# Decode attention over a paged cache: SyncE transfers with page numbers in registers instead of GpSimd's indirect gathers

## The chip, the cores and the metric

The kernel runs on one core of a Trainium2 chip. The metric is the device time of one execution in microseconds. The core has TensorE (PE; its weight loads are PEld), VectorE (DVE), ScalarE (ACT), GpSimd (POOL) and SyncE (SP). SP computes nothing; it issues transfers to the core's 16 DMA engines. Each engine runs its own instructions strictly in the order in which the program holds them.

## The reference

One inference step of a one-layer decoder: a half-step SwiGLU, a token mixer of four GLA heads and four MLA heads, a second SwiGLU. It runs over 1024 prompt tokens and over 8 sample tokens, each with 4096 past tokens in a paged cache. The change concerns the attention of the sample tokens:

```python
past_lat = cache_kv[l, page_table].reshape(B_s, -1, MLA_KV_RANK)   # page: 128 tokens x 128 f32
past_pe = cache_pe[l, page_table].reshape(B_s, -1, MLA_ROPE)       # page: 128 tokens x 64 f32
...
s = (jnp.einsum('bqhc,bkc->bhqk', q_lat, lat_all)
     + jnp.einsum('bqhr,bkr->bhqk', q_pe, pe_all)).astype(jnp.float32) * MLA_SCALE
p = jax.nn.softmax(s, axis=-1)
o_lat = jnp.einsum('bqhk,bkc->bqhc' ...)                           # then w_uv
```

`page_table` has 8 rows of 32 page numbers, drawn from a pool of 320 pages. The sum over past tokens doesn't depend on their order.

## The kernel before, in words

All large products run on TensorE in split precision (`mm3`, L88 to L95, three matmuls for one). The stages follow each other: first SwiGLU, input projection and GLA, attention, output projection (`project`, L1453, which loads w_out by L171), second SwiGLU.

The sample attention is cut into 16 decode units `(g, u)`: group g holds four of the eight sample tokens, u one of eight slices of 512 past tokens. `dec_unit` (L1165) takes four tiles `kvt` (128 partitions x 4 x 128) and four `pet` (128 x 4 x 64), one pair per sample token, from `fetch`; transposes pet (L1176) and kvt (L1184) on TensorE; computes scores (L1189, L1192), softmax (L1162, L1163), the transposes of the probabilities (L1198) and the product with kvt (L1203), which is the last use of kvt. After the units 7 and 15 (counted 0 to 15) `dec_combine` joins the slices, and L1417 applies w_uv.

Tiles come from pools. `bufs=6` at kvt and pet means six buffers for each, so that one unit and half of the next fit; a transfer into a buffer waits for the last reader of what it held.

`decode(2)` issues units 0 and 1 before the prompt attention. Then each of four heads loads its weights (`uqr`, `ukr`, L1289 and L1333, one buffer each), and computes four query blocks: `scores(m)`, then `outputs` of the block before, then `decode(1)`. So each head has four slots, and 14 units fill them. A scheduler of the framework sets the final order of each engine's instructions when the program is built; it moves them past each other where data allows, by priority, free buffers and its own estimates of durations. On the chip the order is fixed. SP's transfers take eight semaphores in turn, and each waits for the one that held its semaphore before, eight transfers back.

Before the change the tiles are filled by `indirect_dma_start` on GpSimd: a tile `idx`, made by DVE (L900 to L902), holds for each of the 128 partitions the row of the cache to fetch. A row is four tokens, and a unit takes such rows from all 32 pages.

Of the kernel before, what the change touches and what calls it, by code (L numbers as in the profile page):

```python
# [10 lines left out]
F32 = mybir.dt.float32  # L11
F32R = mybir.dt.float32r
BF = mybir.dt.bfloat16
I32 = mybir.dt.int32
U8 = mybir.dt.uint8
AF = mybir.ActivationFunctionType
OP = mybir.AluOpType
# [4 lines left out]
P = 128  # L22
# [3 lines left out]
NS = 8  # L26
# [9 lines left out]
PAST = 4096  # L36
NPOOL = 320
# [31 lines left out]
def hybrid_step(ctx: ExitStack, tc: tile.TileContext, I, O, C):  # L69
    nc = tc.nc  # L70
    V, S, PE, GP = nc.vector, nc.scalar, nc.tensor, nc.gpsimd
    ld = nc.sync

    def pool(name, bufs=1, **kw):
        cm = tc.tile_pool(name=name, bufs=bufs, **kw)
        return cm, cm.__enter__()
# [20 lines left out]
    const = ctx.enter_context(tc.tile_pool(name="const", bufs=1))  # L97
# [360 lines left out]
    tiles = [(t * P, P, I["x_prompt"][0, t * P:(t + 1) * P, :]) for t in range(8)] + [(SEQ, NS, I["x_sample"][:, 0, :])]  # L458
# [240 lines left out]
    def bank(name="ps"):  # L699
        return ps.tile([P, 512], F32, name=name, tag="ps")  # L700
# [7 lines left out]
    def mbank():  # L708
        nw[0] += 1
        return (psw, psw, psx)[nw[0] % 3].tile([P, 512], F32, name="pw", tag="pw")  # L710
# [101 lines left out]
    for s in BLKS:  # L812
        n = s.stop - s.start
# [39 lines left out]
    p = bank().rearrange("p (h x) -> p h x", h=8)  # L853
# [4 lines left out]
    for t in range(2):  # L858
        rope(pr, "ropew", qrs[:, t], qs_n[:, 4 + t], P, ss)
        for hh in range(2):  # L860
            a = slice(64 * hh, 64 * hh + 64)
            V.tensor_copy(qpp[0][:64, :, 2 * t + hh], qrs[a, t])
            V.tensor_copy(qpp[1][64:, :, 2 * t + hh], qrs[a, t])
    for h in range(4):
        p = bank()
# [25 lines left out]
    J = 4  # L891
    NU = PAST // (P * J)

    pt = const.tile([P, NS], I32, name="pt")
    for r in range(4):
        ld.dma_start(pt[r:P:4, :], I["page_table"].rearrange("b g -> g b"))
    kb = const.tile([P, NU], I32, name="kb")
    ld.dma_start(kb, C["keybase"])
    idx = const.tile([P, NU, NS], I32, name="idx")
    for u in range(NU):  # L900
        V.tensor_scalar(idx[:, u], pt, P // J, None, op0=OP.mult)
        V.tensor_tensor(idx[:, u], idx[:, u], kb[:, u:u + 1].to_broadcast([P, NS]), op=OP.add)  # L902
    newmask = const.tile([P, 2 * NS], F32, name="newmask")
    ld.dma_start(newmask, C["newmask"])
    kv_rows = I["cache_kv"].rearrange("o n (r k) c -> (o n r) (k c)", k=J)
    pe_rows = I["cache_pe"].rearrange("o n (r k) c -> (o n r) (k c)", k=J)
    fetched = {}

    def fetch(g, u, tiles=None):

        kvt, pet = tiles or ([ep.tile([P, J, P], F32, name="kvt", tag="kvt", bufs=6) for _ in range(4)],
                             [ep.tile([P, J, 64], F32, name="pet", tag="pet", bufs=6) for _ in range(4)])
        for bi in range(4):
            off = bass.IndirectOffsetOnAxis(ap=idx[:, u, 4 * g + bi:4 * g + bi + 1], axis=0)
            for t_, rows in ((kvt[bi], kv_rows), (pet[bi], pe_rows)):
                GP.indirect_dma_start(out=t_.rearrange("p j c -> p (j c)"), out_offset=None, in_=rows, in_offset=off)
        return kvt, pet

    nq = [0]
# [57 lines left out]
    def gla_norm(src, n, gk, tag="on"):  # L977

        ss = gk.tile([P, 8], F32, name="gss", tag="gss")
        on = gk.tile([P, 4, P], F32, name="on", tag=tag, bufs=1)  # L980
        for h in range(4):
            S.activation(on[:n, h], src[:n, h], AF.Square, accum_out=ss[:n, h:h + 1])
        V.tensor_scalar(ss[:n, :4], ss[:n, :4], 1.0 / P, EPS, op0=OP.mult, op1=OP.add)
        GP.tensor_tensor(ss[:n, 4:], ss[:n, :4], mhalf[:n, :4], op=OP.pow)
        for h in range(4):
            if h % 2:
                V.tensor_scalar_mul(on[:n, h], src[:n, h], ss[:n, 4 + h:5 + h])
            else:
                S.activation(on[:n, h], src[:n, h], AF.Copy, scale=ss[:n, 4 + h:5 + h])
        p = bank().rearrange("p (h i) -> p h i", h=4)  # L990
        for h in range(4):
            PE.transpose(p[:, h, :n], on[:n, h], ident[:n, :n])
        return p
# [45 lines left out]
    for c in range(2):  # L1039
# [10 lines left out]
        for t in range(9):  # L1050
            n = P if t < 8 else NS
            ts = slice(t * P, t * P + n)
            p = mbank()
# [66 lines left out]
    p = bank().rearrange("p (h v) -> p h v", h=4)  # L1120
    for h in range(4):
        PE.transpose(p[:NS, h], osn[:, h], ident)
    p = gla_norm(p, NS, gk)
# [23 lines left out]
    def dbank(name="pd"):  # L1147
        return psd.tile([P, 512], F32, name=name, tag="pd")
# [4 lines left out]
    e_cm, ep = pool("dec", 2, side="right")  # L1153
# [6 lines left out]
    def softmax(g, u, sc, n, pout):  # L1160
        stat = grp[g][0]
        V.tensor_reduce(stat[:, 0, u:u + 1], sc[:, :n], AX.X, OP.max, negate=True)  # L1162
        S.activation(pout[:, :n], sc[:, :n], AF.Exp, bias=stat[:, 0, u:u + 1], accum_out=stat[:, 1, u:u + 1])  # L1163

    def dec_unit(g, u):  # L1165

        if u == 0:
            grp[g] = (ep.tile([P, 3, NU + 1], F32, name="stat", tag="stat"), ep.tile([P, NU + 1, P], F32, name="oc", tag="oc", bufs=1))
        oc = grp[g][1]
        kvt, pet = fetched.pop((g, u)) if (g, u) in fetched else fetch(g, u)  # L1170
        sc = dbank("dsc")
        lt, pe = [], []
        for b2 in range(2):
            p = dbank()
            for q in range(4):
                PE.transpose(p[:, q * P:(q + 1) * P],  # L1176
                             pet[2 * b2 + q // 2][:, 2 * (q % 2):2 * (q % 2) + 2, :].rearrange("p j c -> p (j c)"), ident)
            peT = ep.tile([P, 512], F32, name="peT", tag="peT")
            V.tensor_copy(peT, p)
            pe += [peT[:, :256], peT[:, 256:]]  # L1180
        for bi in range(4):
            p = dbank()
            for q in range(4):
                PE.transpose(p[:, q * P:(q + 1) * P], kvt[bi][:, 2 * (q % 2) + q // 2, :], ident)  # L1184
            lt.append(ep.tile([P, 512], F32, name="latT", tag="latT", bufs=4))
            S.activation(lt[bi], p, AF.Copy)
        rows = [slice(32 * bi, 32 * bi + 32) for bi in range(4)]
        for bi in range(4):
            PE.matmul(sc[rows[bi], :], qlp[:, 4 * g + bi], lt[bi], start=True, stop=False)  # L1189
        for par in range(2):  # L1190
            for bi in range(4):
                PE.matmul(sc[rows[bi], par * 256:par * 256 + 256], qpp[par][:, 4 * g + bi], pe[bi], start=False, stop=par == 1)  # L1192
        pp = ep.tile([P, 512], F32, name="dpp", tag="dpp")
        softmax(g, u, sc, 512, pp)
        pT = ep.tile([P, J, P], F32, name="dpT", tag="dpT")
        p = dbank()
        for q in range(4):
            PE.transpose(p[:, q * P:(q + 1) * P], pp[:, q * P:(q + 1) * P], ident)  # L1198
        V.tensor_copy(pT.rearrange("p j q -> p (j q)"), p)
        po = dbank()  # L1200
        for j in range(J):
            for bi in range(4):
                PE.matmul(po[rows[bi], :P], pT[:, (j % 2) * 2 + j // 2, rows[bi]], kvt[bi][:, j], start=j == 0, stop=j == J - 1)  # L1203
        V.tensor_copy(oc[:, u], po[:, :P])
# [42 lines left out]
    def decode(n):  # L1247

        for g, u in units[:n]:
            dec_unit(g, u)  # L1250
            if u == NU - 1:
                dec_combine(g)
        del units[:n]
# [43 lines left out]
    for t in range(2):  # L1297
# [4 lines left out]
        for s in (slice(0, 512), slice(512, SEQ)):  # L1302
            p = bank()
# [3 lines left out]
            for hh in range(2):  # L1307
                a, c = slice(64 * hh, 64 * hh + 64), slice(64 - 64 * hh, 128 - 64 * hh)
# [11 lines left out]
        for j in range(8):  # L1320
            js = slice(j * P, (j + 1) * P)
            p = bank()[:, :256]
# [4 lines left out]
        for hh in range(2):  # L1327
# [9 lines left out]
            for b in range(2):  # L1337
                s = slice(b * 512, b * 512 + 512)
                p = bank()
# [75 lines left out]
    for h in range(4):  # L1415
        p = dbank()
# [23 lines left out]
    for h in range(4):  # L1440
        raw = rawp.tile([P, SEQ], F32, name="yraw", tag="raw")
        i, o = ((2, 0), (2, 256), (2, 512), (2, 768))[h]
# [225 lines left out]
```

## Time and profile before

| | |
|---|---|
| median of three runs | 2166.68 us (2166.26 to 2172.05) |
| the profiled execution | 2166.21 us |
| its span, first to last instruction | 2164.4 us |
| PE busy | 2060.4 us, 95% |
| DVE, ACT, POOL busy | 69%, 39%, 9% |
| transfers issued by SP | 223.35 MB, 33.5% of the engines' time |
| GpSimd's gathers | 25.17 MB, 3.7% |
| mean granted TensorE clock | 0.977 |

Times are microseconds from the first instruction. The busy share of an engine is a mean over stages that differ; a stage is read by its own stretch. "A <- B" in a row of waits means that A stood idle and B's end released it. A granted clock of 1 is 2.4 GHz, the lower of the two levels is 1.2 GHz.

### The profile page before, as it was taken

How to read it: one execution, taken by the hardware profiler on the slowest of the kernel's cores; microseconds unless marked ns; L12 is line 12 of the kernel's file. 1: busy time of each engine (PE TensorE's matmuls, PEld its weight loads, DVE VectorE, ACT ScalarE, POOL GpSimd, SP SyncE). 2: the span in 40 equal slices, each digit the busy share in tenths (PEclk: the TensorE clock that was granted, in tenths of full speed). 3: DMA queues.
4: the chain of work that ended last, by engine and by line, in shares of the span. 5: the costliest groups of instructions: out<-in, count | busy, mean ns of one | idle time of the engine just before them, and what ended most of it. 6: DMA issues, size and time to landing. Idle time of an engine off the chain costs nothing.

```text
span 2164.4 us, 40540 instructions
## 1 busy us (share of the span) xinstructions
PE 2060.4 (95%) x16379; PEld 1934.6 (89%) x16379; DVE 1488.0 (69%) x2918; ACT 841.7 (39%) x1563; POOL 190.7 (9%) x223
## 2 busy tenths in 40 slices
PE   9999999999999999898788888899999999999997
PEld 9999999999999988886456556799999999999997
DVE  7977777785878566664545545577777777776776
ACT  7323223243445223354533534344332232333434
POOL 0000000000000012113343331000000000000000
PEclk9999999999999999998899989999999999999999
DMA  6233233376445221032332232643332332575352
GB/s 215 72 117 94 88 114 93 95 251 208 137 130 150 74 72 30 21 98 79 112 92 81 91 100 62 190 148 113 108 90 88 118 94 86 148 259 168 109 153 94
DMA packets 202220, 251.13 MB, mean 116 GB/s; under 512 B 20240, under 2 KB 162768, under 8 KB 202032
## 3 DMA queue, kind: packets, MB, share of 16 engines
q1 hardware_dynamic: 193840, 223.35, 33.5%
q0 software_dynamic: 8192, 25.17, 3.7%
q8 instruction: 129, 2.11, 0.4%
q14 instruction: 59, 0.48, 0.1%
HBM read 189.18 MB, written 59.30 MB: 115 GB/s over the span
## 4 chain that ended last, share of the span: by engine, by line
PE 86%; DVE 4%; issue 3%; ACT 2%; DMA 2%; POOL 1%; another core or an unknown queue 1%; POOLq 0%; ACTq 0%; DVEq 0%; SPq 0%
PE pp L94 42%; PE pp L410 18%; PE pw L94 6%; PE pr L94 4%; PE pd L1184 2%; PE po L94 1%; PE dsc L1189 1%; PE pw L1059 1%; PE dsc L1192 1%; PE pg L957 1%; PE ps L94 1%; PE pd L1203 1%; DVE qt L953 1%; DMA kvt<-in_cache_kv_dram,idx 1%; PE ps L1399 1%
## 5 line engine op out<-in xcount | busy, mean ns | idle before, releaser
L94 PE MATMUL pp<-bl,ah 128*128 128x260 f32 (+1 forms) x2432 | 688.7, 283 | 1.4 <-DVE bl L86 1.4
L94 PE MATMUL pp<-bh,al 128*128 128x260 f32 (+1 forms) x2432 | 689.4, 284 | 0.2 <-DVE al L86 0.2
L94 PE MATMUL pp<-bh,ah 128*128 128x260 f32 (+1 forms) x2432 | 687.9, 283 | 0.9 <-ACT ah L85 0.5
L94 PEld LDWEIGHTS pp<-bh,ah 128*128 128x128 f32 x2432 | 460.1, 189 | 1.2 <-ACT bh L85 0.6
L94 PEld LDWEIGHTS pp<-bl,ah 128*128 128x128 f32 x2432 | 459.3, 189 | 1.8 <-DVE bl L86 1.8
L94 PEld LDWEIGHTS pp<-bh,al 128*128 128x128 f32 x2432 | 459.5, 189 | 0.4 <-DVE al L86 0.4
L410 PE MATMUL pp<-th,dh 128*128 128x256 f32 (+1 forms) x1232 | 249.1, 283 | 0.1
L410 PE MATMUL pp<-tl,dh 128*128 128x256 f32 x1232 | 248.8, 283 | 0.4 <-DVE tl L86 0.4
L410 PE MATMUL pp<-th,dl 128*128 128x256 f32 x1232 | 248.7, 283 | 0.0
L85 ACT ACTIVATE ah<-raw 128x512 fp32r<-128x512 f32 x208 | 129.0, 628 | 255.8 <-PE pp L94 242.8
L410 PEld LDWEIGHTS pp<-tl,dh 128*128 128x128 f32 x1232 | 190.0, 188 | 2.8 <-DVE tl L86 2.8
L410 PEld LDWEIGHTS pp<-th,dh 128*128 128x128 f32 x1232 | 190.9, 189 | 0.4 <-issue 0.3
L410 PEld LDWEIGHTS pp<-th,dl 128*128 128x128 f32 x1232 | 189.7, 188 | 0.2 <-DVE dl L86 0.2
L86 DVE TENSOR_TENSOR al<-raw,ah 128x512 fp32r<-128x512 f32 x208 | 142.4, 688 | 59.8 <-ACT ah L85 59.8
L85 ACT ACTIVATE dh<-a 128x1024 fp32r<-128x1024 f32 (+1 forms) x84 | 83.0, 988 | 249.4 <-PE pp L410 228.5
L86 DVE TENSOR_TENSOR dl<-a,dh 128x1024 fp32r<-128x1024 f32 (+1 forms) x84 | 95.2, 1133 | 114.7 <-ACT dh L85 108.3
L85 ACT ACTIVATE ah<-sl 128x512 fp32r<-128x512 f32 x132 | 83.1, 631 | 213.7 <-PE pp L94 162.5
L94 PE MATMUL pw<-xh,wh 128*128 128x260 f32 (+4 forms) x320 | 100.5, 314 | 0.0
L94 PE MATMUL pw<-xl,wh 128*128 128x260 f32 (+4 forms) x320 | 99.5, 311 | 0.0
L94 PE MATMUL pw<-xh,wl 128*128 128x260 f32 (+4 forms) x320 | 99.3, 310 | 0.0
L86 DVE TENSOR_TENSOR tl<-traw,th 128x1032 fp32r<-128x1032 f32 (+1 forms) x84 | 95.5, 1137 | 3.2 <-ACT th L85 3.0
L86 DVE TENSOR_TENSOR al<-sl,ah 128x512 fp32r<-128x512 f32 x132 | 90.4, 687 | 7.9 <-ACT ah L85 4.2
(430 smaller groups left out, 3741.6 us busy)
## 6 DMA issues: line engine op xcount, KB each, us to landing
traw<-td SPq DMA_DIRECT2D x70, 516.0 KB
raw<-in_ffn_w_gate_dram SPq DMA_DIRECT2D x52, 512.0 KB
raw<-in_ffn_w_up_dram SPq DMA_DIRECT2D x52, 512.0 KB
a<-in_ffn_w_down_dram SPq DMA_DIRECT2D x40, 512.0 KB
td<-q SPq DMA_DIRECT2D x22, 520.0 KB
td<-q SPq DMA_DIRECT2D x22, 512.0 KB
raw<-in_w_out_dram SPq DMA_DIRECT2D x16, 512.0 KB
td<-q SPq DMA_DIRECT2D x22, 260.0 KB
```

Of the source, the lines that this page charges most:

```text
L85: S.activation(out_h, src, AF.Copy)
L86: eng.tensor_sub(out_l, src, out_h)
L94: PE.matmul(ps, w_, x_, start=i == 0, stop=i == n - 1)
L410: PE.matmul(bank[c][m], w_[:, kk, ms], x_[:, kk, c * N[0]:c * N[0] + N[c]], start=first and j == 0 and (c == 1 or m % 2 == 0), stop=last a ...
L953: V.tensor_mul(qt[pp, :, hh].rearrange("p t (n s) -> p t n s", s=sz), qhi[pp], ehi[pp])
L957: PE.matmul(p[:, t, c], kt[:, t, c * P:(c + 1) * P], qt[:, t, :, c * 64:(c + 1) * 64], start=True, stop=True)
L1059: PE.matmul(p[:n, :256], x_[:, k], w_[:, k % 4, :], start=i == 0, stop=i == 3 * KD - 1)
L1184: PE.transpose(p[:, q * P:(q + 1) * P], kvt[bi][:, 2 * (q % 2) + q // 2, :], ident)
L1189: PE.matmul(sc[rows[bi], :], qlp[:, 4 * g + bi], lt[bi], start=True, stop=False)
L1192: PE.matmul(sc[rows[bi], par * 256:par * 256 + 256], qpp[par][:, 4 * g + bi], pe[bi], start=False, stop=par == 1)
L1203: PE.matmul(po[rows[bi], :P], pT[:, (j % 2) * 2 + j // 2, rows[bi]], kvt[bi][:, j], start=j == 0, stop=j == J - 1)
L1399: PE.transpose(p[:, jj, qi * P:(qi + 1) * P], prs[qi][:, (j + jj) * P:(j + jj + 1) * P], ident)
```

## The change

`idx` and the gathers go. The page table lies in SBUF as it is, 8 x 32. `fetch` now works by whole pages: for each of a unit's four sample tokens and each of four pages, SP loads the page number from SBUF into a register (`value_load`), and issues two transfers with an address made from it, a page of 64 KB into 32 partitions of kvt and one of 32 KB into 32 partitions of pet. That is 32 transfers and 16 register loads per unit, 512 and 256 in all. A unit takes four whole pages per token; tokens are summed in another order. The SP instructions of all pages are chained, so that the scheduler keeps them in the order of the text. Lines after L916 move by 4: L1203 is L1207 in the changed kernel, L1289 is L1293.

```diff
-    pt = const.tile([P, NS], I32, name="pt")
-    for r in range(4):
-        ld.dma_start(pt[r:P:4, :], I["page_table"].rearrange("b g -> g b"))
-    kb = const.tile([P, NU], I32, name="kb")
-    ld.dma_start(kb, C["keybase"])
-    idx = const.tile([P, NU, NS], I32, name="idx")
-    for u in range(NU):
-        V.tensor_scalar(idx[:, u], pt, P // J, None, op0=OP.mult)
-        V.tensor_tensor(idx[:, u], idx[:, u], kb[:, u:u + 1].to_broadcast([P, NS]), op=OP.add)
+    pt = const.tile([NS, PAST // P], I32, name="pt")
+    ld.dma_start(pt, I["page_table"])
...
-    kv_rows = I["cache_kv"].rearrange("o n (r k) c -> (o n r) (k c)", k=J)
-    pe_rows = I["cache_pe"].rearrange("o n (r k) c -> (o n r) (k c)", k=J)
-    fetched = {}
-
-    def fetch(g, u, tiles=None):
-
-        kvt, pet = tiles or ([ep.tile([P, J, P], F32, name="kvt", tag="kvt", bufs=6) for _ in range(4)],
-                             [ep.tile([P, J, 64], F32, name="pet", tag="pet", bufs=6) for _ in range(4)])
+    kv_rows = I["cache_kv"].rearrange("o n (r k) c -> (o n) r (k c)", k=J)
+    pe_rows = I["cache_pe"].rearrange("o n (r k) c -> (o n) r (k c)", k=J)
+    traced, chain = tc.nc.cur_bb.bb.instructions, [None]
+
+    def fetch(g, u):
+
+
+        kvt = [ep.tile([P, J, P], F32, name="kvt", tag="kvt", bufs=6) for _ in range(4)]
+        pet = [ep.tile([P, J, 64], F32, name="pet", tag="pet", bufs=6) for _ in range(4)]
         for bi in range(4):
-            off = bass.IndirectOffsetOnAxis(ap=idx[:, u, 4 * g + bi:4 * g + bi + 1], axis=0)
-            for t_, rows in ((kvt[bi], kv_rows), (pet[bi], pe_rows)):
-                GP.indirect_dma_start(out=t_.rearrange("p j c -> p (j c)"), out_offset=None, in_=rows, in_offset=off)
+            b = 4 * g + bi
+            for a in range(4):
+                first = len(traced)
+                page = ld.value_load(pt[b:b + 1, 4 * u + a:4 * u + a + 1], min_val=0, max_val=NPOOL - 1)
+                for t_, rows_ in ((kvt[bi], kv_rows), (pet[bi], pe_rows)):
+                    ld.dma_start(t_[32 * a:32 * a + 32].rearrange("p j c -> p (j c)"),
+                                 rows_[bass.ds(page, 1)].rearrange("o r c -> (o r) c"))
+                for ins in list(traced[first:]):
+                    if ins.engine == mybir.EngineType.SP:
+                        if chain[0]:
+                            tc.add_manual_dep(ins, chain[0], mybir.DependencyInfo(
+                                mybir.DependencyClass.NoSync, mybir.DependencyReason.DATA), reason="in the order of the text")
+                        chain[0] = ins.name
         return kvt, pet
```

Where SP loads the weights of the heads, its order before has nothing between one head's weights and the next (L1289 and L1333, t = 0 and then t = 1):

```order
L1289 DMA uqr<-in_mla_w_uq_dram 128x2x128
L1333 DMA ukr<-in_mla_w_uk_dram 128x128
L1289 DMA uqr<-in_mla_w_uq_dram 128x2x128
L1333 DMA ukr<-in_mla_w_uk_dram 128x128 x2
L1289 DMA uqr<-in_mla_w_uq_dram 128x2x64 x2
```

After, SP's order at head 1's weights. The bracket names the semaphores waited for: DMAHW the transfer eight before, PE the last reader of the buffer.

```order
L911 TENSOR_LOAD pt
L911 ISA x2
L913 ISA
L913 DMA kvt<-in_cache_kv_dram 32x512 [waits DMAHW4_49]
L913 ISA
L913 DMA pet<-in_cache_pe_dram 32x256 [waits DMAHW5_49]
L1293 DMA uqr<-in_mla_w_uq_dram 128x2x128 [waits DMAHW6_49,DVE_49]
L1337 DMA ukr<-in_mla_w_uk_dram 128x128 [waits DMAHW7_49,DVE_49,Activation_49]
L911 TENSOR_LOAD pt
L911 ISA x2
L913 ISA
L913 DMA kvt<-in_cache_kv_dram 32x512 [waits DMAHW0_49,PE_49]
```

The first six rows are the last page of unit 5; 64 pages, those of units 2 to 5, stand between head 0's weights and these. The same holds for head 2 (units 6 to 9) and head 3 (10 to 13); the last two units' pages, 14 and 15, stand ahead of the loads of ygs, q and w_out for the output projection.

TensorE's order before, around the end of unit 4 (dsc, pd and kvt belong to the decode units, sc, ps and po to the prompt attention):

```order
L1363 MATMUL sc<-k_h,q_h 128x512
L1203 MATMUL pd<-kvt,dpT 32x128 x16
L1364 MATMUL sc<-k_l,q_h 128x512
L1365 MATMUL sc<-k_h,q_l 128x512
L1366 MATMUL sc<-kp_h,qs_12357 128x512
L1367 MATMUL sc<-kp_l,qs_12357 128x512
L1363 MATMUL sc<-k_h,q_h 128x512
L1364 MATMUL sc<-k_l,q_h 128x512
L1365 MATMUL sc<-k_h,q_l 128x512
```

TensorE's order after, from the end of unit 3 to the transposes of unit 5:

```order
L1207 MATMUL pd<-kvt,dpT 32x128 x16
L1180 MATMUL pd<-ident,pet 128x128 x6
L1188 MATMUL pd<-ident,kvt 128x128 x16
L1180 MATMUL pd<-ident,pet 128x128 x2
L1193 MATMUL dsc<-latT,qlp 32x512 x4
L1196 MATMUL dsc<-peT,qpp_8995 32x256 x4
L1196 MATMUL dsc<-peT,qpp_8996 32x256 x4
L1202 MATMUL pd<-ident,dpp 128x128 x4
L1207 MATMUL pd<-kvt,dpT 32x128 x16
L1180 MATMUL pd<-ident,pet 128x128 x6
L1188 MATMUL pd<-ident,kvt 128x128 x16
```

Unit 4 stands whole between units 3 and 5. All of head 0's attention stands ahead of unit 3's transposes of kvt, and head 1's begins behind the scores of unit 5. The same pattern repeats for units 7 to 9 and 11 to 13, and unit 15 stands alone behind all attention. Units 2, 6, 10 and 14 are mixed with attention, as all from 2 on were before; behind it and ahead of the next unit's kvt transposes stand 49, 34, 89 and 74 attention matmuls, of 896 in all four heads.

## Rows read from the trace of the kernel before

**Rows 1.** The page: busy time, and tenths of 40 slices of the span.

```profile
PE 2060.4 (95%) x16379; PEld 1934.6 (89%) x16379; DVE 1488.0 (69%) x2918; ACT 841.7 (39%) x1563; POOL 190.7 (9%) x223
...
PE   9999999999999999898788888899999999999997
...
PEclk9999999999999999998899989999999999999999
```

**Rows 2.** Windows: us, busy time of each engine, granted clock, DMA share, GB/s.

```profile
1026.00:1050.00 24.00, 13.70 (x106) 8.52 (x107) 13.18 (x29) 10.51 (x24) 8.75 (x9) 0.81 0.50 158
...
1026.00:1366.00 340.00, 281.14 (x2235) 203.77 (x2234) 179.51 (x431) 147.46 (x351) 111.64 (x117) 0.91 0.29 88
```

**Rows 3.** TensorE's groups, 1030 to 1366 us: busy us, mean ns.

```profile
L1184 PE MATMUL pd<-ident,kvt 128*128 128x128 f32 x240 | 41.5, 303 | 32.3 <-ACT latT L1186 11.4 <-issue 8.1 <-DMA kvt<-in_cache_kv_dram,idx 7.1
L1189 PE MATMUL dsc<-latT,qlp 128*32 128x512 f32 x121 | 36.0, 770 | 5.7 <-ACT latT L1186 4.2 <-issue 1.5
L1192 PE MATMUL dsc<-peT,qpp 128*32 128x256 f32 x250 | 33.2, 453 | 0.0
...
L1203 PE MATMUL pd<-kvt,dpT 128*32 128x128 f32 x512 | 19.8, 294 | 2.9 <-DVE dpT L1199 2.9
L1176 PE MATMUL pd<-ident,pet 128*128 128x128 f32 x120 | 18.4, 282 | 0.0
...
L1198 PE MATMUL pd<-ident,dpp 128*128 128x128 f32 x64 | 9.9, 278 | 1.5 <-ACT dpp L1163 1.5
```

**Rows 4.** TensorE's waits, 1026 to 1372 us: total us, times, longest.

```profile
PE pd L1184 <- DMA kvt<-in_cache_kv_dram,idx: 7.1, 5, 4.2
...
PE ps L1323 <- DMA kvt<-in_cache_kv_dram,idx: 0.8, 1, 0.8
```

**Rows 5.** GpSimd's timeline: start, us, instruction [idle before <- releaser].

```profile
1247.63 0.95 POOL L916 DMA_INDIRECT kvt<-in_cache_kv_dram,idx  x1 [15.49 <-PE pd L1203]
1248.89 0.95 POOL L916 DMA_INDIRECT kvt<-in_cache_kv_dram,idx  x1 [0.30 <-PE pd L1176]
...
1257.40 0.18 POOL L1443 COPY yraw<-ym_h 1x1 f32<-1x1 f32 x1
```

**Rows 6.** SP's timeline, at the start and around the first units.

```profile
2.54 0.29 SPq L492 DMA_DIRECT2D nws<-in_mix_norm_w_dram  x1
2.87 0.29 SPq L492 DMA_DIRECT2D nws<-in_ffn_norm_w_dram  x1
...
996.46 0.33 SPq L1157 DMA_DIRECT2D uv<-in_mla_w_uv_dram  x1
1026.12 2.43 SPq L1243 DMA_DIRECT2D out_dram<-sd  x4
1028.64 9.42 SPq L1092 DMA_DIRECT2D ygs<-G  x8
...
1041.73 0.43 SPq L801 DMA_DIRECT2D ropew<-const_sin_dram  x1
1042.20 0.43 SPq L800 DMA_DIRECT2D ropew<-const_cos_dram  x1
1042.68 0.43 SPq L801 DMA_DIRECT2D ropew<-const_sin_dram  x1
```

**Rows 7.** TensorE's timeline over units 0 and 1.

```profile
1037.68 1.94 PE L1203 MATMUL pd<-kvt,dpT 128*32 128x128 f32 x32 [2.86 <-DVE dpT L1199]
...
1048.54 1.09 PE L1184 MATMUL pd<-ident,kvt 128*128 128x128 f32 x4 [4.22 <-DMA kvt<-in_cache_kv_dram,idx]
...
1057.61 1.08 PE L1203 MATMUL pd<-kvt,dpT 128*32 128x128 f32 x32
```

**Rows 8.** The chain that ended last, in order of time: start, us, what.

```profile
1204.33 2.89 DMA kvt<-in_cache_kv_dram,idx
...
1365.20 4.08 PE po L94 x21
...
1372.06 28.10 PE pr L94 x114
```

**Rows 9.** The timeline at the last unit's end and at L1417.

```profile
1341.45 1.08 PE L1203 MATMUL pd<-kvt,dpT 128*32 128x128 f32 x32
...
1356.49 0.51 PE L1417 MATMUL pd<-oT,uv 128*128 128x8 f32 x4
```

More of the change, by code (lines that the diff above doesn't have):

```diff
@@ L1169, in dec_unit @@
         oc = grp[g][1]
-        kvt, pet = fetched.pop((g, u)) if (g, u) in fetched else fetch(g, u)
+        kvt, pet = fetch(g, u)
         sc = dbank("dsc")
```

## The prediction, made before the changed kernel ran

> **What bounds the kernel now.** I read the page first, then the stretch in which the cached pages are used, then the queues that feed it. TensorE is busy for 95% of the span and carries the end almost everywhere; only between about 1000 and 1370 us do its slices and its granted clock sag [rows 1]. This stretch holds the 16 decode units, mixed with the prompt attention: 340 us, TensorE busy for 281, clock 0.91 [rows 2]. So TensorE is nearly full there, and it works in a fixed order; what it waits for in that order is lost time.
>
> The six matmul lines of a decode unit sum to 158.8 us in that stretch (41.5 + 36.0 + 33.2 + 19.8 + 18.4 + 9.9), 9.9 per unit [rows 3]; the other 122 us are attention, 30.6 per head. From the last matmuls of unit 1 (1057.6) to those of unit 15 (1341.45) there are 14 steps of 20.3 us [rows 7, 9]. A unit waits little for its pages: 7.1 us in all for kvt and 0.8 for a buffer release put down to it [rows 4]. GpSimd issues a 256 KB gather in 0.95 us, 1.26 from one to the next, so four kvt tiles take 5 us after the unit before has let go of them (PE L1203) [rows 5]. A gather lands 2.9 us after it starts [rows 8]. The gathers hide because attention stands between the units in TensorE's order.
>
> **The change, part by part.**
>
> *Removed.* 128 gathers, 16 DVE instructions that make idx, and four small loads. GpSimd has slack and the DVE instructions run long before the stretch: nothing to gain but the 7.9 us of waits above.
>
> *Added on SyncE.* Per page one register load from SBUF, four register instructions and two transfers (64 KB and 32 KB), 16 pages per unit, 256 in all. Call the time of a page c.
> - Transfers: the issues that stand back to back without a wait repeat every 0.33 us for 4 KB on 8 partitions and every 0.475 for 256 KB on 128 [rows 6]. A page has 32 partitions; I take 0.40, so 0.80 for two (bounds 0.66 and 0.95).
> - Register instructions: nearest is the 0.04 that SP leaves between two issues [rows 6]: 0.2 for four and the semaphore.
> - The register load: no row shows one. Below, the one-element copy by GpSimd, 0.18 [rows 5]; above, the whole round trip of a gather, 2.9 [rows 8]. These ends are far apart; it is a read without a transfer to set up, so I take the geometric middle, 0.72.
>
> c = 0.80 + 0.20 + 0.72 = 1.72 us (bounds 1.0 and 4.05), 27.5 per unit against the 20.3 of a unit today. Each transfer also waits for the one eight before it, four pages back: with 2.9 to land that needs c of 0.73 or more, so it does not bind.
>
> The Trainium skill (DMA: Bandwidth & Descriptors, Latency and other measured facts) puts the floor of a tensor_load at about 600 ns. With it c would be 1.60 and the sum below 2321; no row here shows one.
>
> *Moved.* All pages now stand on SP's queue, in one chain, and the scheduler has laid everything else around them. In SP's order the weights of head 1 (uqr, ukr) stand behind the last page of unit 5, those of head 2 behind unit 9, of head 3 behind unit 13. In TensorE's order, units 3 and 4, 7 and 8, 11 and 12 have no attention matmul between them at all, and 5, 9, 13 and 15 none before their scores. So ten units (3 to 5, 7 to 9, 11 to 13, 15) lose their cover; units 2, 6, 10, 14 keep it.
>
> A bare unit: six buffers hold one and a half units, so at the end of a unit SP may load the last two tiles of the next (8 pages) and the first two of the one after (8 more). The next unit ends after 8c, a landing of 2.9, and its own chain from the last kvt to the last L1203. Unit 1 shows that chain: 1048.54 to 1058.7, 10.2 us, half of it at the lower clock [rows 7]. A bare unit leaves TensorE idle for most of its time; its 32 L1203 records took 1.94 us where the stretch's granted clock was 0.81, with 1.2 GHz in it, and 1.08 at 2.4 GHz later [rows 2, 7], and the transposes of the last pet come behind the last page, so 11.5. A step is the larger of 16c and 8c + 14.4: 27.5 and 28.2. Ten steps: 282.
>
> *The start.* SP gets through one page after the other from 997, is then held by the store of sd (1026.1) and the ygs stores until 1038 as today [rows 6], about 10 pages in. Unit 0 needs 6 more (6c + 14.4 = 24.7; SP has its 24 free slots filled by 14c = 24.1), unit 1 then a step: 1038 + 24.7 + 28.2 = 1090.9, against 1058.7.
>
> *Four stretches of attention*, each up to the end of its covered unit. A head needs TensorE for 30.6 us; before, a head's share of 1058.7 to 1369.4 [rows 7, 8] is 77.7, less the 34.7 of 3.5 units: 43. The attention matmuls behind that unit in the order, 246 of 896, run under the next loads, so three quarters count, and the covered unit's own 9.9: 33 to 42. I take the middle, 38: 152.
>
> *The end.* Combine and output of the last unit: 14 us from its L1203's end to L1417 [rows 9]; then w_out as today. Its weights are now behind 12 loads of q, which run under unit 15.
>
> Sum: 1090.9 + 152 + 282 + 14 = 1538.9, where the first w_out matmul stood at 1372.1 [rows 8]: +166.8. Span 2164.4 + 167 = 2331, and with the 1.8 us around it 2333. The profiled execution took 2166.2, the median of three is 2166.7: no correction.
>
> DMA bytes stay the same (25 MB); the stretch keeps the engines 29% busy [rows 2], so I price nothing there. What would weigh more than this is a unit regaining cover.
>
> **The rivals.**
> - *A page is cheap* (c about 1.0, the low bound). Then 8c + 14.4 = 22.4 sets the step, not SP: 1038 + 20.4 + 22.4 + 152 + 224 + 14 = 1470.8, +99, 2265. For it: SP's shortest issues. Against it: a load that SP must wait for.
> - *A page is dear* (the load costs the full round trip, c 4.05). Step 64.8: 1038 + 56.7 + 46.8 + 152 + 648 + 14 = 1955.5, 2750. At c 2.5 it is 2467.
> - *Not slower: the pages are there when wanted.* Before, TensorE waits only 7.9 us for gathers [rows 4]; smaller transfers without GpSimd could save them: 2158. It needs a step no longer than today's, though without attention in it: with the same start, attention and end, 12 steps must fit in 1372 - 1038 - 14 - 152 = 168, 14.0 each. That is below the 14.4 of landing and chain alone, so attention would have to run under the units, against the order.
> - *No change, 2167: who issues doesn't matter.* For it: GpSimd's issues are hidden today. Against it: 1.26 per 256 KB gather becomes 1.72 per 96 KB page.
>
> The Trainium skill (DMA: Bandwidth & Descriptors, Issuing engines are not separate DMA queues) says that the issuing sequencer's time "is usually small relative to the DMA itself"; this rule would give the last rival. Its rules for kernel authors say the opposite of this change: transfers under 64 KB are mostly overhead, join them. By the rows, the issue is the larger part here.
>
> **How the numbers follow.** Forecast (c from 1.2 to 2.2: 2284 to 2413) 0.72; cheap 0.10; dear 0.12; not slower 0.03; no change 0.03. The predicted time is the likeliest's, 2333. The range takes c from 1.1 to 2.4 (step 23.2 or 38.4: 2274 or 2449), with some 10 us of attention less or more: 2265 to 2460. About 0.3% (6.5 us) is what a measurement can tell from no change: slower 0.94, same 0.03, faster 0.03.
>
> **What would show it.** Right: SP's page groups every 1.6 to 2 us; TensorE's L1207 groups of units 3, 4 and 5 (L1203 before) some 28 us apart with idle time that ends with kvt; uqr of head 1 issued behind unit 5's pages; the first w_out matmul near 1539; the granted clock lower in between. Wrong: pages every 1.2 us or less, or 2.5 and more; or units 20 us apart, which would mean that chain and landing are shorter than I read them; or an attention stretch far from 38 us.

## The result, and the profile of the changed kernel

The changed kernel takes 2277.34 us (median of 4 runs, 2272.59 to 2279.51), the kernel before 2166.55 beside it: a ratio of 1.0502, 95% interval [1.0479, 1.0526]. The direction and the mechanism were as forecast and the time lies in the range; the size was over by 56 us (2333). The profiled execution took 2277.47 us, its span is 2275.6. In two later groups of runs, those of e1 to e4 and of e12, the kernel before took 2109 and 2110 us in all its 7 and 9 runs (the chip of e1 to e4 gave 2166 in the next group); that time was never profiled and its cause is not known, beside it the change would cost some 8%, and the kernels of these groups are compared by their traces and their own times.

The page of the changed kernel, TensorE and its granted clock, answers to [rows 1]:

```profile
PE 2071.7 (91%) x16379; PEld 1932.6 (85%) x16379; DVE 1494.2 (66%) x2902; ACT 846.6 (37%) x1563; POOL 64.5 (3%) x95
...
PE   9999999999999998985857676789999999999997
...
PEclk9999999999999999995868696889999999999999
```

The sag now reaches from slice 18 to slice 26; outside it the page is as before. The windows view, whose columns are those of [rows 2], splits it: from unit 2's end to unit 5's, the three bare steps, and from there to unit 6's end, a stretch with attention.

```profile
1112.45:1188.85 76.40, 42.54 (x319) 26.82 (x318) 18.70 (x38) 15.99 (x35) 0.00 (x0) 0.71 0.23 62
1188.85:1218.90 30.05, 28.93 (x232) 23.44 (x232) 19.62 (x50) 14.32 (x38) 0.00 (x0) 1.00 0.23 63
```

In the bare steps (units without attention beside them in TensorE's order) TensorE works for 42.5 of 76.4 us at a clock of 0.71; in the attention stretch for 28.9 of 30.1 at full clock. What it waits for stands in its timeline (in brackets the idle time ahead and its releaser), from unit 3's end (1134.3) to unit 5's:

```profile
1140.26 0.66 PE L1180 MATMUL pd<-ident,pet 128*128 128x128 f32 x2 [5.55 <-DMA pet<-in_cache_pe_dram]
1146.59 0.66 PE L1180 MATMUL pd<-ident,pet 128*128 128x128 f32 x2 [5.67 <-DMA pet<-in_cache_pe_dram]
...
1161.29 1.72 PE L1207 MATMUL pd<-kvt,dpT 128*32 128x128 f32 x32 [0.78 <-DVE dpT L1203]
...
1172.67 0.66 PE L1180 MATMUL pd<-ident,pet 128*128 128x128 f32 x2 [5.52 <-DMA pet<-in_cache_pe_dram]
...
1187.77 1.08 PE L1207 MATMUL pd<-kvt,dpT 128*32 128x128 f32 x32
```

The transposes of pet (L1180) come tile by tile, the three shown after 5.5 to 5.7 us of idle time, as far apart as four pages of SyncE (6.3 us from 1140.26 to 1146.59). SyncE's timeline shows the pitch of a page:

```profile
1030.12 0.32 SPq L913 DMA_DIRECT2D kvt<-in_cache_kv_dram  x1
1030.62 0.32 SPq L913 DMA_DIRECT2D pet<-in_cache_pe_dram  x1
1031.71 0.32 SPq L913 DMA_DIRECT2D kvt<-in_cache_kv_dram  x1
```

1.59 us from page to page, 1.60 as the median of all 256: so c is 1.60 where the prediction took 1.72. Between the two issues lie 0.50 us, from the second to the next page 1.09, and in that gap the lines of the load (ns: least, median, most):

```profile
L911 SPq TENSOR_LOAD <-pt x256: 262/268/527, 36.5 to 1453.7; - x128
L911 SPq FUSED_REGOPS  x256: 152/152/178, 37.1 to 1454.0; - x128
```

The chain that ended last, between unit 2's end and unit 5's, is SyncE for the most part. The first line is its share by line (L913 the issues, L911 the load); the pieces below are its last on SyncE, before the matmuls of unit 5:

```profile
by line: SPq L913 36.5%; issue 20.5%; SPq L911 19.9%; PE pd L1188 5.5%; ACT latT L1190 3.1%; PE dsc L1193 2.2%; PE ps L94 2.1%; PE pd L1207 2.1%; DMA pet<-in_cache_pe_dram 2.0%; PE dsc L1196 1.1%; ACT dpp L1167 0.9%; PE pd L1180 0.9%; PE pd
...
1170.35 0.32 SPq L913
1170.85 1.57 DMA pet<-in_cache_pe_dram
```

77% is SyncE (36.5 + 20.5 + 19.9; "issue" is time in which it waited for nothing that the profile shows). And it is hardly held up by buffers: from unit 1's end to unit 15's its waits for L1207 are

```profile
SPq L913 <- PE pd L1207: 4.1, 2, 3.9
```

4.1 us in 396.5. Set against the prediction's sum:

| term | predicted | measured | difference |
|---|---|---|---|
| unit 1's end | 1090.9 | 1073.6 | -17.3 |
| four attention stretches | 152 | 135.6 (38.9, 30.1, 36.7, 30.0) | -16.4 |
| ten bare steps | 282 | 260.9 (21.9 to 28.7) | -21.1 |
| last unit to the first w_out matmul | 14 | 19.2 | +5.2 |
| first w_out matmul | 1538.9 | 1489.3 | -49.6 |
| from there to the end of the span | 792.3, as before | 786.3 | -6.0 |

### The profile page after: what moved, and what is told of

Read it like the earlier page. It is cut to its first block, busy times and chain, and to the rows that moved or that the text cites. A ratio compares the mean times of both kernels' runs of the same rounds, so it can differ in the third digit from the quotient of the medians.

```text
span 2275.6 us, 42790 instructions
## 1 busy us (share of the span) xinstructions
PE 2071.7 (91%) x16379; PEld 1932.6 (85%) x16379; DVE 1494.2 (66%) x2902; ACT 846.6 (37%) x1563; POOL 64.5 (3%) x95
## 4 chain that ended last, share of the span: by engine, by line
PE 40%; SPq 7%; issue 3%; ACT 2%; DVE 2%; DMA 0%; POOL 0%; POOLq 0%; ACTq 0%; DVEq 0%
PE pp L94 20%; PE pp L410 9%; SPq L913 4%; PE pr L94 4%; SPq L911 2%; PE po L94 1%; PE pd L1188 1%; PE ps L94 1%; PE ps L1403 1%; PE dsc L1193 1%; PE dsc L1196 0%; PE sc L1367 0%; ACT latT L1190 0%; PE sc L1369 0%; PE pd L1207 0%
## 5 line engine op out<-in xcount | busy, mean ns | idle before, releaser
L1183 DVE COPY peT<-pd 128x512 f32<-128x512 f32 x32 | 22.0, 688 | 143.6 <-PE pd L1180 143.3
```

## The experiments

Three theories were set against each other. P (pace): the stretch lasts as long as SyncE's page count times c, attention included. O (order): only the units without attention cost. L (loop), formed after the first group: a step is at least the pages still to issue after the unit before has let go of its buffers, times c, plus 11 to 14 us of landing and chain; this is the second limit of the prediction's step, 8c + 14.4.

Times are medians. Every edit up to e9 also gives TensorE an order of its own, since the scheduler lays the instructions out anew (e10 to e12 keep e7's). So where e3 and e7 are compared, bare units are compared too, which hold no attention in either order.

**e1: no register load.**

```
-page = ld.value_load(pt[b:b+1, 4*u+a:4*u+a+1], ...)
+page = (b * 16 + 4 * u + a) * 7 % NPOOL      # a constant: rows_[page]
```

> Leaves out the register load: each page's place in the cache is a constant of the program, so SyncE issues the same 512 transfers without the load, its register instructions and the check of bounds (other pages are read, so the decode outputs are those of other pages). Theory P (SyncE's pace): after unit 1 the whole stretch, attention included, lasts as long as SyncE needs for its 224 pages, 1.60 us each in the profile of the changed kernel. Without the load a page should take some 0.75 to 1.0 us, 12 to 16 us per unit, less than the 20.3 of a unit with its attention, so SyncE is no longer the bound and nearly all is given back: 2165 to 2185 us. Theory O (order: a unit without attention beside it costs a fixed landing and chain): with five bare units left (4, 5, 8, 9, 15) at 8 x 0.9 + 14.4 = 21.6 us, and ten others at 9.9 and 122 us of attention, 1073 + 108 + 99 + 122 = 1402 instead of 1470: about 2209 us. Theory I (the transfers' own number and size, not the load): about 2277 us.

The kernel leaves out the page table: it attends to other pages of the same size and number. 2188.51 us (2187.14 to 2191.22). SyncE's timeline, one page after the other:

```profile
1099.72 0.42 SPq L913 DMA_DIRECT2D kvt<-in_cache_kv_dram  x1
1100.18 0.42 SPq L913 DMA_DIRECT2D pet<-in_cache_pe_dram  x1
1100.70 0.36 SPq L913 DMA_DIRECT2D kvt<-in_cache_kv_dram  x1
```

0.93 us per page (median), so two issues cost 0.93 and the load with its register instructions 0.67. Of the 111 us of span, 90 are gone with the same transfers: theory I falls, the load is what costs most. But the steps are 20 to 24 us, outside the two starts of a head pair (33.1, 32.7), and not 14.9 (16 x 0.93): SyncE now waits for the buffers,

```profile
SPq L913 <- PE pd L1207: 86.0, 12, 15.0
```

and a step of 21.5 is 8 x 0.93 + 14.1. P's 2165 to 2185 is just missed, O's 2209 too; steps with and without attention in TensorE's order are equally long. This is where L comes from.

**e2: the load twice.** The value_load line is repeated.

> Each page's register load is done twice, its result the same. The page pitch on SyncE should rise from 1.60 to between 1.9 and 2.35 us. Theory P: the time grows by about 224 to 250 times that rise (0.5 us: 2390 to 2402 us). Theory O: only the ten bare steps grow, by 16 times the rise each, 160 times in all (0.5 us: 2357 us). Theory C (TensorE's lower clock in the stretch is the cost): little change, under 10 us.

2413.47 us. A page now takes 2.19 us:

```profile
1101.23 0.32 SPq L914 DMA_DIRECT2D kvt<-in_cache_kv_dram  x1
1101.75 0.32 SPq L914 DMA_DIRECT2D pet<-in_cache_pe_dram  x1
1103.42 0.32 SPq L914 DMA_DIRECT2D kvt<-in_cache_kv_dram  x1
```

So the second load with its register instructions costs 0.59 us, though its three records last 0.27, 0.15 and 0.02. The Trainium skill (DMA: Bandwidth & Descriptors, Latency and other measured facts) puts the floor of a tensor_load at about 600 ns; the time on the queue agrees, 0.59 here and 0.67 by e1, the record of 0.27 alone does not. The time rises by 136 us over the changed kernel's first median and 142 over e6, that is 231 to 241 per us of c: P's 224 to 250; O's 160 gives 94 and falls, and theory C, under 10 us, with it. The four attention stretches grew as well, from 135.6 to 159.0 (45.7, 35.1, 42.5, 35.7), which O excludes.

**e3: two queues, by halves.**

```
+q_ = ld if bi < 2 else GP
-page = ld.value_load(...)   ...   ld.dma_start(...)
+page = q_.value_load(...)   ...   q_.dma_start(...)
```

> Tiles 0 and 1 of each unit stay with SyncE, tiles 2 and 3 go the same way (register load and two transfers per page) to GpSimd, each queue in the order of its text. SyncE then needs 8 x 1.60 = 12.8 us per unit. Theory P: if GpSimd needs under 2.5 us per page, neither queue is the bound and the time returns to 2165 to 2190 us; if a page takes GpSimd x us over that, it sets the pace itself, 8x per unit. Theory O: units 11 to 15 now stand bare at the end of TensorE's order; five steps of 4 x 1.60 + 14.4 = 20.8 us: about 2200 us.

2220.72 us. GpSimd issues a page every 1.74 to 2.30 us (mean 1.86 within a unit, after unit 1). Neither P's 2165 to 2190 nor O's 2200 came: units with attention beside them in TensorE's order take 23 to 29 us, the bare ones 25 to 29. GpSimd is idle for over 10 us per unit,

```profile
POOL kvt L914 <- PE pd L1208: 126.9, 12, 15.0
...
1157.09 0.50 POOL L914 DMA_DIRECT2D kvt<-in_cache_kv_dram  x1 [0.67 <-issue]
...
1158.83 0.50 POOL L914 DMA_DIRECT2D kvt<-in_cache_kv_dram  x1 [0.67 <-issue]
```

waiting for L1208 (L1207 before the line was added) of the unit before. The two tiles that six buffers leave free early are SyncE's; both that must wait are GpSimd's: the mean step of 25.4 is 8 x 1.86 + 10.5.

**e4: the heads' weights from ScalarE's queue.** In uq_tile and for ukr, `ld.dma_start` becomes `S.dma_start`.

> Only the weights of the heads (uqr, ukr) are issued by ScalarE's queue instead of standing behind pages in SyncE's queue; the pages stay as they are. Theory P: SyncE loses four short groups of loads (some 3 us each), nothing else: 2260 to 2270 us. Theory Q (head-of-line: what costs is that the attention's weights stand behind the pages, which takes the cover from the units): the attention is free of the pages and most of the loss is given back, 2190 us or less.

2271.68 us (2270.32 to 2276.62), as e6 below. Q falls. TensorE's order is quite another (units 5 to 8 in a row without attention, and 14 and 15), yet unit 1's end to unit 15's takes 392.5 us against 396.5: with SyncE as the pacer it does not matter where the attention stands. P's saving on SyncE's other loads is 4 us there, less than expected, and the time is 2 us above its 2270.

**e5 and e6: both kernels again.**

> The kernel before, unchanged, for its trace on the chip of this group of runs. In the group e1 to e4 the kernel before took 2109 us where the trace that the prediction rests on stands in a run of 2166 us. If a chip runs all kernels faster, every stretch shortens; if one stretch alone differs (the decode stretch, or the granted clock in one place), its windows show it.

> The changed kernel, unchanged, beside the kernel before on the same chip. If its decode stretch is paced by SyncE, it takes 2270 to 2280 us on any chip, whatever the kernel before takes there; if the chip is faster as a whole, some 2220 us.

2162.22 us (span 2160.4; unit 1 to 15 in 284.0, before 283.8), so this trace does not show the 2109; and 2271.53 (397.5 for 396.5; ratio 1.0496, interval [1.0465, 1.0527]). Both traces repeat the first ones to 1.5 us in the 14 steps and in the part from w_out on. Unit 1's end they don't repeat as well: 1056.3 for 1058.7, and 1068.1 for 1073.6, so differences of some 5 us there can't be told from chance.

**e7: two queues, alternating.** As e3, with `q_ = ld if bi % 2 == 0 else GP`.

> As e3, but SyncE fetches tiles 0 and 2 of each unit and GpSimd tiles 1 and 3. In e3 the two tiles for which a buffer was free early were both SyncE's, and the two that wait for the unit before both GpSimd's, so GpSimd's 8 pages (1.75 to 1.92 us each) stood behind every unit's end. Theory L (loop: a unit's step is at least the pages still to issue after the unit before has let go of its buffers, times the page's pitch on their queue, and about 14 us for landing and chain, as e1 with 8 x 0.93 + 14 = 21.5 showed): now 4 pages of each queue stand there, 4 x 1.9 + 14 = 21.6, about 2180 us, near e1. Theory P (only the pace of a queue counts): each queue needs 8 x 1.9 = 15.2 us per unit, as in e3, so no change against e3: 2215 to 2225 us.

2149.48 us, a ratio of 0.9931 [0.9906, 0.9955]. P falls: each queue has the same 8 pages as in e3, but 71 us are gone, 62 of them in the 14 steps. TensorE's order differs too (units 14 and 15 bare here, 11 to 15 in e3), but the bare units alone took 20.4 and 22.3 us here and 25.2 to 29.2 in e3. L's step was 21.6; the mean is 21.0 (294.1 us for 14 steps). The time came out 30 us below L's, since against the kernel before unit 1 ends 12.6 us sooner, the first w_out matmul follows unit 15's end after 19.7 us instead of 29.5, and what follows takes 6.0 less (e12 is on this last part).

**e8: five buffers.** `bufs=6` becomes 5 for kvt and pet.

> The changed kernel with five buffers of kvt and pet instead of six, all else the same: one tile less can be loaded ahead. Theory L: after a unit's end 12 pages have still to be issued, 12 x 1.60 + 14 = 33.2 us per step against 28.3 on average now (396.5 us for 14 steps): about 70 us more, 2345 us. Theory P (SyncE's pages alone set the pace, the buffers stalled it for 4 us in all): at most 2290 us.

2318.08 us, ratio 1.0709 [1.0682, 1.0735]; 47 us more than e6, between the two. The mean step is 31.1 (435.1 for 14), 12 x 1.60 + 11.9. SyncE's wait shows the new bound:

```profile
SPq L913 <- PE pd L1207: 48.6, 14, 8.2
```

Once per unit, against two waits in all with six buffers: so L is right in kind, its 14 was too long for this kernel, and P alone, which gave at most 2290, falls. The constants of 10.5 to 14.1 are what is left of each run's mean step, not separate measurements. At six buffers both limits lie together: 16 x 1.60 = 25.6 and 8 x 1.60 + 11 to 14 = 24 to 27. More than six were not tried.

**e9: kv from SyncE, pe from GpSimd.** Each engine loads the page number for itself.

```
+for q_, t_, rows_ in ((ld, kvt[bi], kv_rows), (GP, pet[bi], pe_rows)):
+    page = q_.value_load(...); q_.dma_start(...)
```

> SyncE loads each page's number and issues its kv transfer; GpSimd loads the same number for itself and issues the pe transfer. A page costs SyncE the load block and one issue, some 1.1 us (1.60 less the 0.50 between its two issues), and GpSimd about as much; the buffers of pet come free with the transposes of pet, earlier than those of kvt. Theory L (loop): the 8 kv pages that wait for a unit's end take 8.8 us, then landing and chain without the transposes of pet, some 11 to 13 us: steps of 20 to 22, 2150 to 2170 us. Theory P (pace alone): 17.6 us per unit on either queue, below the 20.3 of a unit with its attention: 2140 to 2150 us, as low as e7 or lower.

2171.19 us, ratio 1.0021 [1.0004, 1.0037]; mean step 21.9 (305.9 for 14). L gave steps of 20 to 22 and 2150 to 2170; P's 2140 to 2150 falls. L holds in the step, and the time is 1 us above its range. A page of kv alone costs SyncE 1.1 us, 8 x 1.1 + 13.1.

**e10: pages on SyncE, gathers on GpSimd.** Tiles 0 and 2 as in e7, tiles 1 and 3 with the index table and the gathers of the kernel before.

> Tiles 0 and 2 of each unit by pages on SyncE as in e7, tiles 1 and 3 by the indirect gathers of the kernel before on GpSimd (one per tile and cache). TensorE's order is that of e7. Behind a unit's end GpSimd now has 2 gathers instead of 4 pages, some 2.5 us instead of 7; SyncE still has 4 pages, 6.4 us. Theory L: SyncE's 6.4 + 14 = 20.4 stays the step, so as e7, 2143 to 2152 us. If GpSimd's part set the pace in e7 (4 x 1.8 = 7.2 against 6.4), up to 0.8 us per step or 11 us less: 2138 us.

2165.65 us, ratio 0.9998 [0.9984, 1.0012]: outside both ranges. The stretch is as in e7 (296.7 against 294.1 for 14 steps), as L said, but unit 1 ends at 1058.5 instead of 1046.1 and from the first w_out matmul to the end 793.6 us pass instead of 786.4. Both lie outside the pages' stretch.

**e11: e7 again.**

> The kernel of e7 once more, in more rounds, beside the kernel before: 2145 to 2155 us, and a ratio to the kernel before of 0.991 to 0.995 if its lead holds.

2152.15 us, ratio 0.9945 [0.9924, 0.9967]: the lead holds.

**e12: e7 with its constants as large as before.**

```
-pt = const.tile([NS, PAST // P], I32, name="pt")
+pt = const.tile([NS, PAST // P + 48], I32, name="pt")   # 192 bytes unused
...   (the load fills the first PAST // P columns)
```

> The kernel of e7 with 192 unused bytes per partition behind the page table, so that its constants take 320 bytes there, as in the kernel before and in e10, and not 128 (as in the changed kernel and all others); every engine's instructions and their order are those of e7, only the places of the later tiles in SBUF move. In the traces the kernels with 128 bytes have 3049 TensorE instructions in the 360 us from 120 us after the first w_out matmul, those with 320 bytes 3010, and e10 also reaches unit 1's end 11 us later than e7 under nearly the same order. Theory S (places in SBUF): 3010 instructions here too, and 6 us more behind w_out: 2158 us; with the 11 us of the start 2169 us, so that the lead of e7 over the kernel before is not due to pages at all. Theory G (the gathers themselves, or the work around them): unchanged, 3049 instructions and 2148 to 2156 us.

2165.50 us (2164.29 to 2166.26), 13 to 16 more than e7 and e11, with the same instructions in the same order on every engine. Windows of 360 us, 120 us after the first w_out matmul, first of e7, then of e12 (PE's instructions in the first brackets, its clock after POOL's):

```profile
1479.90:1839.90 360.00, 360.00 (x3049) 360.00 (x3048) 275.08 (x556) 113.58 (x203) 0.00 (x0) 1.00 0.33 102
```

```profile
1489.30:1849.30 360.00, 360.00 (x3010) 360.00 (x3009) 270.71 (x544) 112.96 (x200) 0.00 (x0) 1.00 0.34 101
```

TensorE is full and at full clock in both, but a matmul comes every 118.1 ns in one and every 119.6 in the other. All ten traces of kernels with 128 bytes of constants there show 3048 to 3050 instructions in such a window, and 786.3 to 788.7 us from the first w_out matmul to the end; the four with 320 bytes (the kernel before, e5, e10, e12) show 3010 or 3011, and 791.0 to 793.6 us. Theory G falls, and S holds in kind.

The span is 16.3 us longer than e7's: 6.6 at unit 1's end (1052.7), 2.7 in the 14 steps, 0.2 behind them, 6.9 from w_out on. The last of these is borne out by all the traces; the 6.6 at the start are hardly more than two traces of one kernel differ by there (e6), so they are not shown to come from the bytes. So the tail of the table above, -6.0, is not the pages' doing, and with the bytes kept the pages would cost 117 us, or 124 if the 6.6 at the start count too (an estimate, 111.2 + 6.0 and + 6.6). Without its smaller constants nothing is left of e7's lead: padded it takes 2165.5, as e10 with the same bytes does, and as the kernel before did beside e7 and e10. But e12 ran once, in another group than they, and beside it the kernel before took 2110 (ratio 1.0261). The kernel before was not run with 128.

## Why the prediction was right, and where its size was off

- *What bounds it, and that cover is lost.* Right. TensorE's idle time in the bare steps ends with pet (12 waits, 53.1 us, from unit 1's end to unit 15's; the prediction named kvt, but each page's pet is issued 0.50 us behind its kvt), the chain runs through SyncE, and moving half of SyncE's pages elsewhere (e7) gives the loss back. The rule that the issuing sequencer's time "is usually small relative to the DMA itself" (the Trainium skill, DMA: Bandwidth & Descriptors, Issuing engines are not separate DMA queues) does not hold for this kernel: same bytes, 122 us less in e7 than in e6.
- *c.* 1.60 for 1.72. Two errors cancel in part: the two issues were taken at 0.80 and cost 0.93 (e1), the load with its register instructions at 0.92 and cost 0.67 (e1) or 0.59 (e2).
- *The bare step, "the larger of 16c and 8c + 14.4".* Both limits are real: e2 follows the first (36.1 us, mean of the ten, for 16 x 2.19 = 35.0), e1 and e8 the second. 14.4 is too much for the changed kernel. Its trace shows landing and chain directly, from the issue of a unit's last page to the unit's end; for unit 4 from here to 1163.01, the end of the L1207 group at 1161.29 above, 11.8 us:

```profile
1151.23 0.32 SPq L913 DMA_DIRECT2D pet<-in_cache_pe_dram  x1
```

In nine of the ten bare units it is 10.0 to 12.6 us (15.3 in unit 15). The prediction let the second limit decide, with 28.2; with c at 1.60 and 11.8 for 14.4 the second gives 24.6 and the first 25.6, and the measured mean is 26.1: -21.1 over ten steps, the largest part of the miss. That SyncE waits for buffers only twice (4.1 us) shows the first limit at work.
- *The four attention stretches, 38 each.* Mis-sized as one number. Units 2 and 10 begin a pair of heads, with its rope, queries and values, and took 38.9 and 36.7; units 6 and 14 begin the second head of a pair and took 30.1 and 30.0, with TensorE busy for 28.9 in either. The prediction shared out the attention evenly. By the prediction's own sign of being wrong, a stretch far from 38 us, the term fails for those two.
- *The start, "held until 1038 as today".* This step failed. SyncE's timeline has the last ygs stores end at 1027.6, not at 1038 [rows 6], so pages ran 10 us sooner:

```profile
1025.76 1.81 SPq L1096 DMA_DIRECT2D ygs<-G  x4
1028.46 0.34 SPq L913 DMA_DIRECT2D kvt<-in_cache_kv_dram  x1
```

Of unit 1's -17.3, these 10 us and c (22 pages x 0.12 = 2.6) account for some 13, an estimate; e6 came another 5.5 us sooner. Why the stores end earlier is not shown: fewer decode matmuls stand ahead of their inputs in TensorE's order, which is an argument only.
- *The end.* 19.2 for 14: TensorE waits 9.1 us for the first w_out block. The 12 loads of q did run under unit 15, as predicted (the last is issued at 1467.3), but behind them SyncE stands at the load of yrs (L1451) until DVE has split yraw, whose buffer yrs takes next, and w_out is issued only then. SyncE's wait, and the landing of w_out in the chain:

```profile
SPq L1451 <- DVE yg_l L86: 14.9, 1, 14.9
...
1484.15 4.04 DMA raw<-in_w_out_dram
```

- *Weights behind pages.* The order was as said, but it was not a cause of its own: e4 takes them away and gains 6 us on the first runs of the changed kernel and nothing on e6.
- *The clock.* It fell to 0.71 in the bare steps, where TensorE was idle for 34 of 76 us; e2, with more idle time, follows SyncE's pitch, so the clock is no bound here.
- *Rivals.* "Not slower" needed steps of 14.0; even e1, without the load, has 20. For "a page is cheap" the prediction gave 2265 us at c = 1.0, but e1 took 2188.5 at 0.93: the sum kept ten bare steps and added the attention to them, and with cheap pages most attention stands within the steps, as in e1's order. The same sum gives 2411 us at e2's c of 2.19, where 2413 were measured, 2321 at 1.60 for 2277, and some 2258 at e1's 0.93 for 2188.5: it is too high the more, the cheaper the page. That it fits so well at 2.19 is partly luck, since unit 1's end is 16 us over there and the attention 7 under.

## What to carry to other kernels

Before work moves to a queue, count what that queue must issue per unit, times the measured pitch of the whole sequence (load, register instructions, issues), against the time of a unit; here 16 x 1.60 against 20.3 decided. Then count only those transfers that must wait for a buffer, add landing and chain, and split just these between queues: e3 and e7 differ in their source in nothing but which tiles each queue has, and by 71 us. And when a change also resizes what stands in SBUF, run one kernel with the old size: 192 bytes went with 13 to 16 us here, as much as the lead of the best version.

## What the runs showed of the hardware

- 192 bytes more or less per partition among the constants, which move the later tiles in SBUF, change TensorE's pace at full clock with the same instructions: 119.6 against 118.1 ns per matmul (e12, e7; all 14 traces fall in line). Which tile's place does it is open.
- A register load on SyncE adds 0.59 us to the queue, though its records sum to 0.44; a page with its load costs 1.60 on SyncE (the changed kernel) and 1.75 on GpSimd (e7).
- Two constant-address transfers of 32 partitions cost 0.93 us, while behind a load the same two issues last 0.32 each with 0.50 from one to the next.
